# Two-layer hybrid block on one core: order of elements in a triangular inverse, and where partial sums are kept

## Chip, cores and metric

One core of a Trainium2 chip runs the whole program in one launch. The metric is the device time in microseconds, the median of several runs. Engines are named as in the profile: PE (TensorE matmul; PEld is its weight load), DVE (VectorE), ACT (ScalarE), POOL (GpSimd), SP (SyncE, which here only issues DMAs).

## What is computed

Two layers over 512 latent and 256 context tokens of width 1024. In each layer one input projection feeds three token mixers (bidirectional RWKV-7, latent attention, windowed attention), each of them gated, projected and merged:

```python
h = rms_norm(x, norm_g) * (1.0 + scale) + shift
za, ga, zb, gb, zc, gc, zg = jnp.split(h @ w_in, list(IN_CUTS), axis=-1)
# RWKV-7: S <- S diag(w) - (S kk)(kk*a)^T + v k^T ; y = S r, over time, both directions
ya, yb, yc = rwkv(za), attention(zb), window_attention(zc)
gates = sigmoid(zg)                                  # three branches x 1024 channels
m = sum(gates[n] * ((y[n] * silu(g[n])) @ w_branch_out[n]) for n in range(3))
x = x + gate * (m @ w_out)
```

The context tokens take the same way in the first layer; the second gives only the latent tokens. All is fp32.

## The kernel before

Activations lie with channels on partitions and T = 768 tokens (256 context, 512 latent) along the free axis. A matrix product splits both operands into a high part (fp32r) and a rest and adds three products (`hh,wh`, `hl,wh`, `hh,wl`), 512 and 256 columns wide. ScalarE makes the high part of the weights (L165), GpSimd the rest (L166).

The order is made by a planner: every instruction has a priority by its `band` (a lower number goes first), and the planner places it on its in-order engine by its own estimate of durations. `SERVE` is the first band; in layer 0 the scan has band 1, the heads 3, the filler 4, the end of the layer 5. A layer runs so:

1. `head` normalises; `zphase` makes the RWKV inputs and writes them to memory (`ard`, `bkd`, `vd`, and `ttd` for the triangular matrices).
2. `rwkv` scans 12 chunks of 64 tokens, 16 (head, direction) pairs at once. Groups of NS = 4 chunks share one `rwkv_inverse`, which inverts unit triangular 32x32 blocks: load `TT`, transpose (L666), mask on GpSimd (L670), 30 steps of a product and a sum on VectorE (L676, L678), two transposes (L681, L682), then small matmuls `zp` and `yp` that join two blocks to 64x64. It is a generator; `yield` marks where the caller may do something else. The inverse of group 0 stands before the scan; that of a later group is advanced at the end of each chunk of the group before, and in three steps in its last chunk. `rwkv_step` is the chain from chunk to chunk: `Rp`, `Up` (which needs `YB`, the inverse), `Sp`, with copies `UV` and the state `So` on VectorE and ScalarE. `rwkv_scores` prepares the chunk after next (`scps`, `AR`, `TR`).
3. `pace(n)` advances the filler, `tiles`, by n steps: the other projections (`zb`, `ga`, `gb`, `zc`, `gc`, then 24 of the merge gates), 8 steps to a tile; a tile of `g` kind ends in a SiLU on VectorE (`st`, L779). `FILL[l]` says how many steps stand around `zphase`, before the scan, and in each part of a chunk; `readout` runs after chunks 3, 9 and 11 and reads `ga`. What is left of the filler (`gates`) stands behind the attention heads in priority.
4. `mla` and `gqa`, the attention heads.
5. In layer 0, `later(0)` and `later(1)` run branches 0 and 1 of the merge, and `tail` branch 2 and the output product. `branch` loads a gated mixer output (`ygt`), splits it into `yh` and `yl`, multiplies by `w_bo`, and per tile of 128 channels loads the gates (`zt`), and VectorE makes the product (L1356). Branch 0 writes it to `md` in memory; branch 1 loads it back (`m`, L1364), adds (L1365) and writes the sum (L1366); `tail` loads that (L1381) and adds (L1382). Tiles `xs`, the residual stream on chip for the next layer, are allocated just before `tail`.

Pools are stacked: `bo` (with `yh`, `yl`, `ygt`, `zt`, `m0`) is opened where `hh` and `hl` were, after their last use. The next layer's conditioning (`modps`, `mod`) is interleaved with the filler, too.

Of the kernel before, what the change touches and what calls it, by code (L numbers as in the profile page):

```python
# [19 lines left out]
P = 128  # L20
# [9 lines left out]
GB, RB, CB = 2, 3, 2  # L30


FILL = ((48, 36, 2, (2, 2, 2), (3, 3, 3), 2), (72, 56, 4, (2, 2, 2), (3, 3, 3), 2))

QUEUES = (("scalar", "sync", "sync", "scalar"), ("sync", "scalar", "sync", "sync"))

# [24 lines left out]
def build(tc, A, out):  # L61
# [448 lines left out]
    def rwkv(l, D, last, DL, B, pace, zlast):  # L510

        with tc.tile_pool(name="rw", bufs=1, reuse_waits="tile") as rp:
            yo = rp.tile([P, 4, T], F32, name="yo")
            st = {"seen": set(), "S": None}
            parts, YB = {}, {}

            def scores(i):
                if i < NCH:
                    parts[i] = yield from rwkv_scores(l, last, rp, i)

            def invert(g):
                if g < NG:
                    YB[g] = rp.tile([P, 32, 64], F32, tag="YB", name="YB", bufs=2)
                    yield from rwkv_inverse(l, rp, g, YB[g])

            def rest(*gens):
                for g in gens:
                    for _ in g:
                        pass

            with band(B + 1):
                rest(scores(0), scores(1))
                ahead = invert(0)
                for _ in range(3):
                    next(ahead)
            with band(B + 4), tc.issue_after(zlast):
                pace(FILL[l][1])
            with band(B + 1), in_line():
                for _ in ahead:
                    pace(FILL[l][2])  # L540
                ahead = out = iter(())
                for i in range(NCH):
                    if i % NS == 0:
                        rest(ahead)
                        ahead = invert(i // NS + 1)
                    nxt = scores(i + 2)
                    step = rwkv_step(l, last, i, yo, st, DL, rp, parts.pop(i), YB[i // NS])
                    for n in FILL[l][3 if i % NS < NS - 1 else 4]:
                        next(step, None)
                        next(nxt, None)  # L550
                        if i % NS == NS - 1:
                            next(ahead, None)
                        next(out, None)
                        pace(n)
                    rest(step, nxt)
                    if i % NS < NS - 1:
                        next(ahead, None)
                    if i in READY and (i > 3 or not last):
                        rest(out)
                        out = readout(l, D, rp, yo, READY[i])  # L560
                for _ in out:
                    pace(FILL[l][5])

# [90 lines left out]
    def rwkv_inverse(l, rp, g, YB):  # L654
# [3 lines left out]
        for b0 in (0, 64):  # L658

            DMA.dma_start(TT[b0:b0 + 32], tt_d[l][b0:b0 + 32, :, cs])  # L660
            DMA.dma_start(TT[b0 + 32:b0 + 64, :, :, 0:32], tt_d[l][b0 + 32:b0 + 64, :, cs, 32:64])
        inv = rp.tile([P, 1536], F32, tag="inv", name="inv")
        MB, tmp = inv[:, 0:1024], inv[:, 1024:1536]
        YK = YB[:, :, 32:64]
        TT4 = TT.rearrange("p c s t -> p (c s) t")
        V.transpose(MB, TT4[:, :, 0:32].rearrange("p n j -> p j n"))  # L666

        M3 = MB.rearrange("p (j i) -> p i j", i=32)
        Y3 = YK.rearrange("p j i -> p i j")
        G.affine_select(YK, MB.rearrange("p (j i) -> p j i", i=32),  # L670
                        [[1, 32], [-1, 32]], ALU.is_gt, 0.0, base=0, channel_multiplier=0)
        V.memset(YB.rearrange("p n c -> p (n c)")[:, 32:2048:65], 1.0)
        for j in range(30, 0, -1):
            n = 31 - j
            t3 = tmp[:, 256 * (j % 2):256 * (j % 2) + j * n].rearrange("p (i c) -> p i c", c=n)
            V.tensor_tensor(t3, M3[:, 0:j, j:j + 1].to_broadcast([P, j, n]),  # L676
                            Y3[:, j:j + 1, j + 1:32].to_broadcast([P, j, n]), ALU.mult)
            V.tensor_tensor(Y3[:, 0:j, j + 1:32], Y3[:, 0:j, j + 1:32], t3, ALU.add)  # L678
            if j in (22, 12):
                yield  # L680
        V.transpose(YB[:, :, 0:32].rearrange("p n j -> p j n"), YK)  # L681
# [646 lines left out]
        turns(8, prepare, attend, later, filler)  # L1328


    def branch(l, n_, tp, segs, bank, put, lead=()):

        yh, yl = ({s0: tp.tile([P, 4, n], F32R, tag=f"{t}{s0}", name=t, bufs=1) for (s0, n) in segs} for t in ("yh", "yl"))
        with band(SERVE):
            for j in range(4):
                for (s0, n) in segs:
# [12 lines left out]
        for j in range(8):  # L1349
            yield  # L1350
            ps = finish(begun[j]) if j < len(lead) else gemm(A["w_bo"][l, n_, j], 4, yh, yl, segs, bank)
            with band(SERVE):
                for (s0, n), p_ in zip(segs, ps):
                    th = tp.tile([P, 512], F32, tag="zt", name="zt", bufs=4 if l else 5)[:, 0:n]
                    DMA.dma_start(th, th_zg[l][8 * n_ + j][:, s0:s0 + n])
                    V.scalar_tensor_tensor(th, th, 1.0, p_, ALU.add, ALU.mult)  # L1356
                    put(j, s0, n, th)

    def early(l, n_, tp, segs):

        def put(j, s0, n, t):
            if n_:
                m0 = tp.tile([P, 512], F32, tag="m0", name="m0", bufs=3)[:, 0:n]
                DMA.dma_start(m0, m_d[l][j][:, s0:s0 + n])  # L1364
                (G if l else V).tensor_tensor(t, t, m0, ALU.add)  # L1365
            DMA.dma_start(m_d[l][j][:, s0:s0 + n], t)  # L1366

        return branch(l, n_, tp, segs, "gg", put)

    def tail(l, mod, last, xs, bp):  # L1370
        segs = (LAT,) if last else (LAT, CTX)
        with tc.tile_pool(name="tailp", bufs=1, reuse_waits="tile") as tp:
# [4 lines left out]

            def put(j, s0, n, t):
                sl = slice(s0, s0 + n)
                m0 = tp.tile([P, 512], F32, tag="m0", name="m0", bufs=3)[:, 0:n]  # L1380
                DMA.dma_start(m0, m_d[l][j][:, sl])  # L1381
                V.tensor_tensor(t, t, m0, ALU.add)  # L1382
                S.copy(mh[:, j, sl], t)  # L1383
                V.tensor_tensor(ml[:, j, sl], t, mh[:, j, sl].bitcast(F32), ALU.subtract)
# [38 lines left out]
    for l in range(2):  # L1423
# [18 lines left out]
        def tiles():  # L1442
# [2 lines left out]
            zc = [(T_ZC + j, zb_d[l][4 + j], (LAT,) if last and j < 4 else BOTH, "raw") for j in range(6)]  # L1445
            ga, gb, gc = ([(t + j, g_d[l][4 * n + j], segs, "silu") for j in range(4)]
                          for n, t in enumerate((T_GA, T_GB, T_GC)))
            todo = zb[2:] + zc[4:] + zc[:4] + zb[:2] + ga + gb if last else zb + ga + gb + zc
            todo += gc + [(T_ZG + j, th_zg[l][j], segs, "tanh") for j in range(24)]
            for a in todo:  # L1450
                yield from proj(l, hh, hl, *a, side)
# [37 lines left out]

        def later(n_):  # L1490

            g = early(l, n_, bp, segs)
            with band(B + 4):
                next(g)
            for _ in range(8):
                yield
                with band(B + 4):
                    next(g, None)
# [35 lines left out]
        if not last:  # L1534
            gates()
            bp = merge_pool()
            for n_ in range(2):
                for _ in later(n_):
                    pass
# [1 line left out]
            for _ in chain(*fillers):  # L1541
                pass
        with band(B + 5):
            if not last:
                xctx = ExitStack()
                xp = xctx.enter_context(tc.tile_pool(name="xs", bufs=1, side="right"))
                xs = [xp.tile([P, T], F32, name=f"xs{k}") for k in range(KT)]
            weights["queue"] = getattr(nc, QUEUES[l][3])
            tail(l, mod, last, xs, bp)
            bctx.close()  # L1550
# [95 lines left out]
```

## Time and profile before

| | us |
|---|---|
| median of 3 runs | 2393.21 |
| lowest, highest | 2389.98, 2396.64 |
| profiled execution, its own time | 2389.18 |
| its span, first to last instruction | 2387.5 |

| engine | busy us | share |
|---|---|---|
| PE | 2104.1 | 88% |
| DVE | 1303.6 | 55% |
| ACT | 891.0 | 37% |
| POOL | 867.3 | 36% |

A share is a mean over stages. Layer 0 scans from about 415 to 680 us, runs its heads to about 1165 and merges to about 1303; layer 1 scans from about 1700 to 1920. To read a stage, take the busy time of its stretch, then PE's waits in it. PE's granted clock is given as a share of the full one.

### The profile page before, as it was taken

The numbers are of one execution on the slowest core, as the hardware profiler recorded it, in microseconds if no ns is written. First come the engines' busy times: TensorE is split into PE (matmuls) and PEld (weight loads), VectorE is DVE, ScalarE is ACT, GpSimd is POOL, SyncE is SP. The second block draws the span as 40 slices with busy tenths as digits, with TensorE's granted clock in tenths as the row PEclk, the third lists the DMA queues.
The fourth block names the chain that finished last, engine by engine and source line by source line (L and its number), as shares of the span: only waits on it lengthen the run. The fifth ranks groups of instructions, "written<-read, shape, count | busy, mean of one in ns | idle before, by whom it ended". The sixth has DMA issues, their size and how long they took to land. (4 is left out here: it accounts for less than half of the span.)

```text
span 2387.5 us, 42421 instructions
## 1 busy us (share of the span) xinstructions
PE 2104.1 (88%) x16680; PEld 1624.5 (68%) x16680; DVE 1303.6 (55%) x2300; ACT 891.0 (37%) x1654; POOL 867.3 (36%) x699
## 2 busy tenths in 40 slices
PE   6986895987998999989888998789868998999989
PEld 3865674766887766766677876567646876666657
DVE  4475326766337666247435255733678347566643
ACT  3443211233345333454213244433222356434432
POOL 1354312111123345444433324544211135556663
PEclk9998898998999999999999999999888999999999
DMA  7146575555241111531487414467444253215344
GB/s 251 58 135 183 181 199 146 150 139 134 72 161 54 67 34 54 183 98 38 142 264 227 148 56 124 137 210 189 122 110 113 82 181 105 92 49 181 107 146 145
DMA packets 330441, 314.23 MB, mean 132 GB/s; under 512 B 112768, under 2 KB 239488, under 8 KB 330240
## 3 DMA queue, kind: packets, MB, share of 16 engines
q1 hardware_dynamic: 312432, 281.87, 39.7%
q10 hardware_dynamic: 17808, 29.63, 3.9%
q8 instruction: 132, 2.16, 0.4%
q14 instruction: 69, 0.57, 0.1%
HBM read 213.64 MB, written 97.78 MB: 130 GB/s over the span
## 5 line engine op out<-in xcount | busy, mean ns | idle before, releaser
L166 POOL TENSOR_TENSOR wl<-wf,wh 128x512 fp32r<-128x512 f32 x316 | 425.9, 1350 | 1026.3 <-ACT wh L165 928.5
L154 PE MATMUL g<-hh,wh 128*128 128x512 f32 (+1 forms) x1264 | 469.9, 372 | 19.5 <-DVE st L779 10.9
L154 PE MATMUL g<-hh,wl 128*128 128x512 f32 (+1 forms) x1264 | 455.9, 361 | 2.1 <-POOL wl L166 2.0
L154 PE MATMUL g<-hl,wh 128*128 128x512 f32 (+1 forms) x1264 | 454.7, 360 | 0.0
L165 ACT CAST wh<-wf 128x512 fp32r<-128x512 f32 x316 | 195.1, 619 | 467.3 <-PE g L154 238.3
L154 PEld LDWEIGHTS g<-hh,wh 128*128 128x128 f32 x1264 | 248.7, 197 | 67.9 <-DVE st L779 12.8
L154 PEld LDWEIGHTS g<-hh,wl 128*128 128x128 f32 x1264 | 248.7, 197 | 41.4 <-issue 7.7
L154 PEld LDWEIGHTS g<-hl,wh 128*128 128x128 f32 x1264 | 249.2, 197 | 37.0 <-issue 8.7
L889 POOL TENSOR_TENSOR acc<-acc,pe 128x512 f32<-128x512 f32 (+2 forms) x128 | 145.2, 1135 | 117.0 <-ACT pe L885 97.5
L885 ACT ACTIVATE pe<-stp 128x256 f32<-128x256 f32 (+2 forms) x224 | 114.7, 522 | 187.6 <-PE stp L154 179.0
L867 DVE TENSOR_REDUCE mx<-mps 128x1 f32<-128x384 f32 (+2 forms) x256 | 124.7, 533 | 59.1 <-PE mps L154 58.2
L676 DVE TENSOR_TENSOR inv<-inv,YB 128x30 f32<-128x30 f32 (+9 forms) x180 | 90.9, 505 | 8.5 <-issue 2.3
L154 PE MATMUL yps<-pe,vh 128*64 128x256 f32 (+1 forms) x704 | 94.8, 379 | 0.1
L154 PE MATMUL g<-yh,wh 128*128 128x512 f32 (+1 forms) x224 | 81.9, 369 | 13.0 <-DVE zt L1356 6.6
L678 DVE TENSOR_TENSOR YB<-YB,inv 128x30 f32<-128x30 f32 (+9 forms) x180 | 90.4, 502 | 5.3
L154 PE MATMUL g<-yl,wh 128*128 128x512 f32 (+1 forms) x224 | 83.2, 372 | 8.5 <-POOL yl L1341 8.5
L909 DVE RECIPROCAL rec<-sps 128x256 f32<-128x256 f32 (+1 forms) x48 | 70.3, 1478 | 33.6 <-PE sps L154 33.4
L154 PE MATMUL gc<-hh,wh 128*128 128x512 f32 x192 | 77.1, 401 | 8.6 <-ACT hh L325 4.5
L889 POOL TENSOR_TENSOR acc<-pe 128x512 f32<-128x512 f32 (+1 forms) x48 | 53.7, 1118 | 83.0 <-ACT pe L885 73.9
L777 ACT ACTIVATE st<-g 128x256 f32<-128x256 f32 (+1 forms) x108 | 56.6, 524 | 71.1 <-PE g L154 70.1
L154 PE MATMUL g<-yh,wl 128*128 128x512 f32 (+1 forms) x224 | 80.5, 363 | 0.0
L642 DVE TENSOR_TENSOR AR<-scps,cst 64x256 f32<-64x256 f32 x96 | 40.1, 418 | 72.0 <-PE scps L154 70.9
(386 smaller groups left out, 4364.8 us busy)
## 6 DMA issues: line engine op xcount, KB each, us to landing
wf<-w_in SPq DMA_DIRECT2D x163, 256.0 KB, 2.9
wf<-ada_w SPq DMA_DIRECT2D x84, 256.0 KB, 4.1
wf<-w_in ACTq DMA_DIRECT2D x77, 256.0 KB, 2.9
bkd<-bk SPq DMA_DIRECT2D x16, 768.0 KB, 6.3
zt<-thzg SPq DMA_DIRECT2D x48, 256.0 KB, 3.6
wf<-w_bo SPq DMA_DIRECT2D x40, 256.0 KB, 2.8
thzg<-st SPq DMA_DIRECT2D x24, 384.0 KB, 2.4
md<-zt SPq DMA_DIRECT2D x32, 256.0 KB, 3.3
```

The costliest lines, as they stand in the source:

```text
L154: queued(TE.matmul(o, l, r, start=start, stop=stop, **kw))
L165: S.copy(wh, w32)
L166: eng.tensor_tensor(wl, w32, wh.bitcast(F32), ALU.subtract)
L642: V.tensor_tensor(AR[oth, pds, 2 * par, :], ps[oth, :, a0:a0 + 64], msk("ms", oth), ALU.mult)
L676: V.tensor_tensor(t3, M3[:, 0:j, j:j + 1].to_broadcast([P, j, n]), Y3[:, j:j + 1, j + 1:32].to_broadcast([P, j, n]), ALU.mult)
L678: V.tensor_tensor(Y3[:, 0:j, j + 1:32], Y3[:, 0:j, j + 1:32], t3, ALU.add)
L777: S.activation(t[:, sl], p, AF.Tanh, scale=0.5)
L867: V.tensor_reduce(mx, ps, AX.X, ALU.max)
L885: S.activation(e, st, AF.Exp, scale=scale)
L889: G.tensor_tensor(acc, keep.pop(0, acc), e, ALU.add)
L909: V.reciprocal(rec, sps)
```

## The change

1. The inverse's inner loop runs over i, which is contiguous, where it ran over c, which is 64 words apart in `YB`. The operand that is broadcast along the inner dimension changes from the matrix to the row factor.
2. `rwkv_inverse` yields once more, after its loads. The next group's inverse is created at the group's start, its loads at the scan's priority, its VectorE part in band B+2 at once; the call at the end of each chunk goes.
3. `FILL` of layer 0 has 48 steps before the scan where it had 36, and `zc` goes ahead of `ga` and `gb` in layer 0.
4. In layer 0 the sums of the three branches are kept in `xs`, which is now allocated before the merge: branch 0 writes its product there, branch 1 adds, `tail` reads. The traffic over `md` is gone there.
5. `yh` and `yl` have two buffers in layer 0.

```diff
-FILL = ((48, 36, 2, (2, 2, 2), (3, 3, 3), 2), (72, 56, 4, (2, 2, 2), (3, 3, 3), 2))
+FILL = ((48, 48, 2, (2, 2, 2), (3, 3, 3), 2), (72, 56, 4, (2, 2, 2), (3, 3, 3), 2))
...
                 ahead = invert(0)
-                for _ in range(3):
+                for _ in range(4):
                     next(ahead)
...
                         rest(ahead)
+
                         ahead = invert(i // NS + 1)
+                        next(ahead, None)
+                        with band(B + 2):
+                            for _ in range(3):
+                                next(ahead, None)
...
-                    if i % NS < NS - 1:
-                        next(ahead, None)
...
             DMA.dma_start(TT[b0 + 32:b0 + 64, :, :, 0:32], tt_d[l][b0 + 32:b0 + 64, :, cs, 32:64])
+        yield
...
-        M3 = MB.rearrange("p (j i) -> p i j", i=32)
-        Y3 = YK.rearrange("p j i -> p i j")
+        M3 = MB.rearrange("p (j i) -> p j i", i=32)
...
-            t3 = tmp[:, 256 * (j % 2):256 * (j % 2) + j * n].rearrange("p (i c) -> p i c", c=n)
-            V.tensor_tensor(t3, M3[:, 0:j, j:j + 1].to_broadcast([P, j, n]),
-                            Y3[:, j:j + 1, j + 1:32].to_broadcast([P, j, n]), ALU.mult)
-            V.tensor_tensor(Y3[:, 0:j, j + 1:32], Y3[:, 0:j, j + 1:32], t3, ALU.add)
+            t3 = tmp[:, 256 * (j % 2):256 * (j % 2) + j * n].rearrange("p (c i) -> p c i", c=n)
+            V.tensor_tensor(t3, M3[:, j:j + 1, 0:j].to_broadcast([P, n, j]),
+                            YK[:, j + 1:32, j:j + 1].to_broadcast([P, n, j]), ALU.mult)
+            V.tensor_tensor(YK[:, j + 1:32, 0:j], YK[:, j + 1:32, 0:j], t3, ALU.add)
...
-    def branch(l, n_, tp, segs, bank, put, lead=()):
+    def branch(l, n_, tp, segs, bank, put, lead=(), into=None):
-        yh, yl = ({s0: tp.tile([P, 4, n], F32R, tag=f"{t}{s0}", name=t, bufs=1) for (s0, n) in segs} for t in ("yh", "yl"))
+        yh, yl = ({s0: tp.tile([P, 4, n], F32R, tag=f"{t}{s0}", name=t, bufs=1 if l else 2) for (s0, n) in segs}
+                  for t in ("yh", "yl"))
...
-                    V.scalar_tensor_tensor(th, th, 1.0, p_, ALU.add, ALU.mult)
-                    put(j, s0, n, th)
+                    to = into(j)[:, s0:s0 + n] if into else th
+                    V.scalar_tensor_tensor(to, th, 1.0, p_, ALU.add, ALU.mult)
+                    put(j, s0, n, to)
...
+        def add(j, s0, n, t):
+            if n_:
+                V.tensor_tensor(sums[j][:, s0:s0 + n], sums[j][:, s0:s0 + n], t, ALU.add)
...
+        if sums:
+            return branch(l, n_, tp, segs, "gg", add, into=None if n_ else sums.__getitem__)
...
-                m0 = tp.tile([P, 512], F32, tag="m0", name="m0", bufs=3)[:, 0:n]
-                DMA.dma_start(m0, m_d[l][j][:, sl])
+                if last:
+                    m0 = tp.tile([P, 512], F32, tag="m0", name="m0", bufs=3)[:, 0:n]
+                    DMA.dma_start(m0, m_d[l][j][:, sl])
+                else:
+                    m0 = xs[j][:, sl]
...
-            todo = zb[2:] + zc[4:] + zc[:4] + zb[:2] + ga + gb if last else zb + ga + gb + zc
+            todo = (zb[2:] + zc[4:] + zc[:4] + zb[:2] if last else zb + zc) + ga + gb
...
             bp = merge_pool()
+            xctx = ExitStack()
+            xp = xctx.enter_context(tc.tile_pool(name="xs", bufs=1, side="right"))
+            xs = [xp.tile([P, T], F32, name=f"xs{k}") for k in range(KT)]
             for n_ in range(2):
                 for _ in later(n_):
                     pass
```

## Rows read from the trace of the kernel before

**Rows 1.** The page, engines: busy us, share of the span, instructions.

```profile
PE 2104.1 (88%) x16680; PEld 1624.5 (68%) x16680; DVE 1303.6 (55%) x2300; ACT 891.0 (37%) x1654; POOL 867.3 (36%) x699
```

**Rows 2.** Busy time by stretch: stretch, length, engines with instructions, granted clock, DMA.

```profile
440.00:480.00 40.00, 32.77 (x418) 26.02 (x412) 37.23 (x78) 9.34 (x20) 5.18 (x4) 0.91 0.61 162
600.00:640.00 40.00, 39.67 (x751) 34.77 (x751) 16.33 (x35) 13.41 (x25) 5.14 (x4) 1.00 0.24 74
1080.00:1120.00 40.00, 39.39 (x300) 26.87 (x300) 29.75 (x48) 17.85 (x44) 16.95 (x18) 1.00 0.15 44
1172.00:1303.00 131.00, 113.26 (x572) 93.42 (x573) 56.24 (x90) 30.77 (x60) 53.61 (x47) 0.91 0.82 258
```

**Rows 3.** PE's waits, 376 to 416 us: total us, times, longest.

```profile
PE zp L154 <- DVE inv L682: 23.3, 1, 23.3
```

**Rows 4.** PE's waits, 440 to 600 us, scan of layer 0.

```profile
PE modps L154 <- DVE mod L272: 6.3, 3, 3.1
PE modps L154 <- DVE mod L269: 4.1, 1, 4.1
PE Rp L154 <- DVE UV L714: 4.0, 1, 4.0
```

**Rows 5.** PE's waits, 1640 to 1720 us, ahead of layer 1's scan.

```profile
PE g L154 <- DVE st L779: 10.3, 3, 4.8
PE zp L154 <- issue: 4.7, 1, 4.7
```

**Rows 6.** PE's waits, 1720 to 1880 us, scan of layer 1.

```profile
PE zp L154 <- DVE inv L682: 16.5, 2, 13.9
PE scps L154 <- DVE TR L644: 9.6, 3, 4.1
```

**Rows 7.** PE's waits, 1172 to 1303 us, merge of layer 0.

```profile
PE g L154 <- DVE zt L1356: 6.6, 5, 3.0
PE g L154 <- ACT yh L1340: 6.3, 5, 4.9
PE g L154 <- POOL yl L1341: 4.7, 10, 1.6
PE gc L154 <- DVE zt L1356: 3.7, 1, 3.7
```

**Rows 8.** Timeline of DVE: start, us, engine, line, operation, out<-in, shapes.

```profile
379.58 0.15 DVE L676 TENSOR_TENSOR inv<-inv,YB 128x30 f32<-128x30 f32 x1 [0.35 <-DVE st L779]
379.77 0.19 DVE L678 TENSOR_TENSOR YB<-YB,inv 128x30 f32<-128x30 f32 x1
462.57 0.69 DVE L739 TENSOR_TENSOR So<-So,DL 128x512 f32<-128x512 f32 x1
464.27 0.60 DVE L676 TENSOR_TENSOR inv<-inv,YB 128x240 f32<-128x240 f32 x1
464.91 0.62 DVE L678 TENSOR_TENSOR YB<-YB,inv 128x240 f32<-128x240 f32 x1
1678.32 1.50 DVE L676 TENSOR_TENSOR inv<-inv,YB 128x238 f32<-128x238 f32 x1
```

**Rows 9.** DVE busy in the first inverse: L676, then L678.

```profile
379.40:412.20 32.80, 15.03 (x30) 0.76 0.65 148
379.40:412.20 32.80, 14.66 (x30) 0.76 0.65 148
```

**Rows 10.** PE in a 5 us stretch: busy, granted clock, DMA.

```profile
415.00:420.00 5.00, 4.53 (x76) 0.50 0.00 0
```

**Rows 11.** DMA from 1172 to 1303 us: total, and one group of issues.

```profile
DMA packets 24025, 33.85 MB, mean 258 GB/s; under 512 B 2667, under 2 KB 12159, under 8 KB 24017
md<-zt SPq DMA_DIRECT2D x16, 256.0 KB, 4.0
```

**Rows 12.** Timeline of PE in the filler: start, us, operation, shape.

```profile
341.36 0.40 PE L154 MATMUL g<-hh,wh 128*128 128x512 f32 x1
341.60 0.40 PE L154 MATMUL g<-hl,wh 128*128 128x512 f32 x1
```

More of the change, by code (lines that the diff above doesn't have):

```diff
@@ L1355, in branch, with early @@
                     DMA.dma_start(th, th_zg[l][8 * n_ + j][:, s0:s0 + n])
-                    V.scalar_tensor_tensor(th, th, 1.0, p_, ALU.add, ALU.mult)
-                    put(j, s0, n, th)
-    def early(l, n_, tp, segs):
+                    to = into(j)[:, s0:s0 + n] if into else th
+                    V.scalar_tensor_tensor(to, th, 1.0, p_, ALU.add, ALU.mult)
+                    put(j, s0, n, to)
+    def early(l, n_, tp, segs, sums):
+        def add(j, s0, n, t):
+            if n_:
+                V.tensor_tensor(sums[j][:, s0:s0 + n], sums[j][:, s0:s0 + n], t, ALU.add)
         def put(j, s0, n, t):
@@ L1490, in later @@
         def later(n_):
-            g = early(l, n_, bp, segs)
+            g = early(l, n_, bp, segs, () if last else xs)
             with band(B + 4):
@@ L1543, in build @@
         with band(B + 5):
[L1544 to L1547, printed above, removed]
             weights["queue"] = getattr(nc, QUEUES[l][3])
```

## Prediction

> **What bounds the kernel now.** The page comes first: PE is busy for 2104 of 2387.5 us [rows 1], so only two things can shorten the span by much: PE's idle stretches and stretches at the lower clock. The busy time by stretch then says where these lie. While the scan runs without an inverse on VectorE, PE is full (39.7 of 40 us at 600) with VectorE at 16.3 of 40; while an inverse runs beside it (440), VectorE is at 37.2 and PE at 32.8; the attention heads at 1080 are full again, and the merge of layer 0 (1172 to 1303) has PE at 113 of 131 us [rows 2]. Third, PE's waits in those stretches name who is late. Ahead of the first scan PE stands once for 23.3 us, on the last transpose of the inverse [rows 3]. In the scan of layer 0 it waits for small VectorE results (`mod`, `UV`) that are queued among the inverse's instructions, 14.4 us in three groups [rows 4]. Layer 1 repeats it: 10.3 us for the SiLU of the filler projections (`st`) and 4.7 us before the first scan [rows 5], 16.5 us for the inverse and 9.6 us for `TR` within it [rows 6]. In the merge it waits for the products with the gates (6.6 and 3.7 us) and for split rows (4.7 us) [rows 7].
>
> **Inverse, cost of one.** Its 30 steps have j(31-j) elements each, j from 30 to 1, 4960 in all, in two instructions (L676 multiplies, L678 adds). Before, the inner dimension walks c, 64 words apart in `YB`. A 240-element step took 0.60 and 0.62 us; a 30-element one with j = 30, whose elements are already neighbours, 0.15 and 0.19; a 512-element operation with neighbouring elements and an inner broadcast (L739) 0.69 [rows 8]. From 0.17 at 30 to 0.69 at 512 is 1.08 ns an element and 0.138 us fixed. New sum: 4960 x 1.08 ns = 5.4 us plus 30 x 0.138 = 4.1 us, 9.5 us for one kind, 19.0 for both. The first inverse has 15.03 + 14.66 = 29.7 us in them [rows 9]. **Each of six inverses loses about 10.7 us.** Bounds: 0 (the inner broadcast, now on the other operand, eats it) to 12. L739 has just such a broadcast and no surcharge, hence 10.7. Some steps take an extra 0.9 us, such as 1.50 us for 238 elements [rows 8]; I leave these in.
>
> Here the trace speaks against a page. The 240-element steps cost 0.2 us more than the neighbouring-element line gives (0.138 + 240 x 1.08 ns = 0.40 us) [rows 8]. The Trainium skill, "VectorE: DVE Perf Modes", section "Mode 1× (REGULAR) — the baseline", says that mode takes one result a cycle and works with any stride; by that rule the reordering would give nothing. The row decides for me, and the rule is the first rival below. For the slow steps, the skill's "SBUF — State Buffer", section "Who interferes with whom", says that a VectorE instruction with two SBUF inputs contends with GpSimd's reads; the new order would not change that, and the sum has no gain from it.
>
> **Ahead of the first scan, layer 0.** `FILL` moves 12 of the filler's steps here. A step is three 512-wide and three 256-wide matmuls; at a pitch of 0.24 us and, as an estimate, half that for the narrow ones [rows 12], 1.05 us, so 12.6 us. Inverse 10.7 shorter plus 12.6 more filler equals the 23.3 us wait [rows 3]. The two are not alike: 10.7 is off the path at once; the other 12.6 comes back only where the filler is taken away, in the attention heads, and there only while PE is the bound. It is at 39.4 of 40 us at 1080 [rows 2], but its idle gaps earlier in the heads don't shrink, so I count 70%, 9 us. **-20 us** (-10 to -23). The raw projections `zc` before the gates `ga` also take SiLU instructions off VectorE here; counted as nothing. `ga` ends after 112 filler steps, and 48+48+4+27 = 127 are out when the first readout needs it; if it were late it would cost one tile, 8.4 us, once.
>
> **Scan, layer 0.** Two inverses at 10.7 us leave a VectorE that was 93% busy [rows 2], and the inverse now stands at a lower priority (B+2) than the scan's own operations. What PE waits for here is queued behind it: 14.4 us [rows 4], of which I take three quarters, **-11 us** (0 to -14). Next late is the `AR` load. The earlier load I count as nothing: no wait in [rows 4] is on `TT`. Its four DMA issues now stand ahead of a chunk's loads on SP.
>
> **Layer 1.** Before the scan the path is the inverse; PE's 15 us [rows 5] are bounded by its 10.7: **-10 us** (0 to -15). In the scan the next inverse starts a chunk earlier and is 10.7 shorter; the 16.5 us wait should go nearly whole, and half of the 9.6 on `TR` [rows 6]: **-20 us** (-8 to -26). Each `zp` behind the inverse has `yp` and then all of the scan's `Up` waiting for it.
>
> **Merge of layer 0.** 32 writes and 32 reads of partial sums leave the SP queue and memory: 8 rows of 384 KB, four passes, 12.6 MB of the 33.9 MB that this stretch moves at 258 GB/s [rows 11]. Branch 0 multiplies straight into `xs`; the additions stay on VectorE. PE's own work is three branches of eight tiles, 12 x 0.24 + 12 x 0.12 = 4.3 us each [rows 12], 104 us in a stretch of 131. Waits of 6.6, 4.7 and 3.7 us [rows 7] are 15 us; reads and stores in front of the gates' loads and the single buffer of `yh`, `yl` cause them. **-15 us** (+10 to -25). The lower end is nearly all of 131 - 104. The upper is for the room: hh and hl free 48 KB a partition; the old pool is 24 + 8 + 10 + 6 = 48, the new one 48 + 8 + 10 = 66, so its `ygt` and `zt` now lie where the window attention's tiles were, and `xs` where its keys were. Their first loads wait, on SP, for the last head, and I price that at twice the 4.9 us that PE waits for the first `yh` now [rows 7].
>
> **Clock.** After a long wait PE's clock is granted at half (1.2 of 2.4 GHz), and the 4.5 us of work from 415 on ran so [rows 10]. Some seven waits of this size fall away or shrink; at 1 to 2 us each I take **-5 us** (0 to -15).
>
> **Sum.** -20 -11 -10 -20 -15 -5 = -81 us. Span 2387.5 to 2306.5; the profiled run is 1.7 us longer than its span, so 2308, against its own 2389.18. The median is 4 us above that run, so at its level **2312 us**.
>
> **Rivals.**
> *Strides are free, the inverse stays at 30 us.* For: the six inverses have other delays in them too. Against: 0.60 us beside the 0.40 of the line [rows 8]. Then the filler (9), the merge (15), and 8 of layer 1's scan for the earlier start remain: 32 us, **2361**. This is what the skill's rule above would give.
> *The pool's overlap takes back the merge.* For: 66 KB against 48. Against: branch 0 can't start before the filler's last tile frees hh, today either. +10 in place of -15, with the clock half gone: -54, **2339**.
> *The scan starves the inverse.* It stands behind every scan operation on VectorE; where it isn't finished by the last chunk of a group of four, PE stops at the boundary, at the 23.3 us of the one such wait that the trace has [rows 3]: four boundaries, +93; with -50 from the rest (20, 10, 15, 5) that is +43, **2436**, slower. It decides where a group leaves less VectorE free than the 19 us of an inverse. Against it: without inverse 24 of 40 us are free, and twelve chunks run from 418 to past 640 [rows 2, 3], 75 us or more for four, so some 45.
> *The gain of the scan turns into another wait* (loads of `AR`, ScalarE's copies): B and layer 1's scan give 10 instead of 31; -60, **2333**.
>
> **How the numbers follow.** Forecast 0.60; strides free 0.12; overlap 0.12; another wait 0.08; starvation 0.08. The range 2278 to 2368 reaches from 115 us down, where nearly all the favourable ends meet (-23 -14 -15 -26 -25 -15 = -118), to the strides-free case with 7 us on top; starvation and about 0.1 of the tails are left out. 0.3% is 7 us, about what a measurement here tells from no change. Slower is starvation, 0.08; the tail of the strides and overlap cases near 2393 is 0.05; faster 0.87.
>
> **What would show it.** L676 and L678 at a mean near 0.32 us, from 0.505 and 0.502. The 23.3 us wait on the inverse gone; if it has become 10 or more, the filler is short. VectorE in the scan's first 40 us below 32. Waits for `st` in layer 1 under 4 us. No `md` traffic in layer 0, the merge near 115 us, PE's first wait in it no longer than 5. If the inverse shortens and the scan does not, the scan's own chain was the bound. If PE idles more in the attention heads of layer 0, the moved filler is missed there.

## The result and the profile after

The changed kernel takes **2353.1 us** (2352.7 to 2359.8) against 2392.5 us: ratio 0.9845 [0.9829, 0.9862], 39 us less. The forecast was 2312, so the sign held and less than half of the 81 us came. The profiled execution has a span of 2351.5 us. One execution among all those of this study, of the variant with the old sums through memory, took 4867.8 us and is left out of that variant's figures.

Five views of after answer to rows of before. The page's engines [rows 1]: PE lost 7 us of busy time, VectorE 36.

```profile
PE 2096.9 (89%) x16680; PEld 1623.2 (69%) x16680; DVE 1267.4 (54%) x2300; ACT 890.7 (38%) x1654; POOL 865.6 (37%) x699
```

Busy time by stretch, columns as in [rows 2] (stretch, length, then PE, PEld, DVE, ACT and POOL with their instructions, granted clock, DMA share, GB/s), the last stretch being the merge of layer 0:

```profile
440.00:480.00 40.00, 27.22 (x343) 21.72 (x342) 34.76 (x85) 8.70 (x16) 4.57 (x4) 0.87 0.58 129
600.00:640.00 40.00, 39.89 (x700) 34.53 (x702) 16.80 (x36) 12.75 (x24) 5.75 (x5) 1.00 0.28 81
1080.00:1120.00 40.00, 39.25 (x289) 26.79 (x290) 30.31 (x47) 20.10 (x50) 17.79 (x19) 1.00 0.18 50
1155.00:1289.00 134.00, 110.86 (x625) 94.25 (x622) 67.45 (x104) 33.94 (x67) 57.89 (x50) 0.91 0.54 167
```

In the scan's first stretch PE fell from 32.8 to 27.2 us: it waits there more than before, 6.3 us for loads of `AR` and 6.3 for `mod`. PE's waits over whole stages name the reason. The lines come from five stretches (376 to 416, 440 to 600, 1640 to 1700, 1690 to 1850, 1155 to 1289 us) and answer to [rows 3 to 7] in turn:

```profile
PE zp L154 <- DVE inv L685: 2.3, 1, 2.3
...
PE scps L154 <- DMA AR<-ard: 13.5, 3, 7.2
PE modps L154 <- DVE mod L272: 6.6, 3, 6.1
...
PE zp L154 <- issue: 6.4, 1, 6.4
PE g L154 <- DVE st L782: 4.3, 2, 3.1
...
PE zp L154 <- DVE inv L685: 12.9, 2, 10.8
PE Rp L154 <- ACT UV L716: 3.9, 2, 2.5
PE scps L154 <- DVE TR L647: 2.2, 2, 2.0
...
PE g L154 <- ACT yh L1345: 17.7, 1, 17.7
PE g L154 <- DVE zt L1362: 3.5, 1, 3.5
PE g L154 <- POOL yl L1346: 1.7, 4, 0.7
```

Two waits have grown. The scan of layer 0 waits 13.5 us for loads of `AR` (3.7 before), and the merge's first matmul waits 17.7 us for a split row (4.9 before). The 23.3 us ahead of the first scan are nearly gone, yet that scan starts at 411.0 us, only 4.5 us earlier: filler has taken the place of the wait.

DMA in the merge [rows 11] fell from 33.85 to 22.37 MB, as the diff promised:

```profile
DMA packets 16078, 22.37 MB, mean 167 GB/s; under 512 B 1791, under 2 KB 8133, under 8 KB 16069
```

For the rest of the document the profiled executions are cut at five marks of PE's timeline: the first `zp` of each layer's scan, the first `krp` behind each scan, and the first `mh` matmul of layer 0. "Tail" is the time from the filler's last matmul to that `mh` and is part of the column before it. All in us; the columns without the tail add up to the span. The profiled execution of "order only" took 2360.2 us, 8 more than its median, so its stages hold some us that most of its executions do not have.

| kernel | to scan 0 | scan 0 | heads and merge 0 | (tail) | mh to scan 1 | scan 1 | rest |
|---|---|---|---|---|---|---|---|
| before | 415.5 | 293.7 | 594.8 | 136.0 | 396.2 | 255.4 | 431.9 |
| after | 411.0 | 294.0 | 583.6 | 161.7 | 388.4 | 238.9 | 435.6 |
| old element order | 420.8 | 308.1 | 587.2 | 162.2 | 395.9 | 252.5 | 435.2 |
| order only | 410.6 | 286.3 | 599.5 | 138.6 | 390.4 | 236.7 | 434.9 |
| 36 steps | 409.9 | 286.9 | 580.0 | 126.8 | 390.1 | 235.3 | 438.6 |
| 36 steps, single | 406.9 | 288.5 | 588.3 | 127.5 | 389.0 | 239.0 | 434.2 |
| 36 steps, single, queue | 401.4 | 282.1 | 581.8 | 125.3 | 390.0 | 236.8 | 437.2 |

### The profile page after: what moved, and what is told of

It reads as the page before. It is cut to its first block, busy times and chain, and to the rows that moved or that the text cites. A ratio compares the mean times of both kernels' runs of the same rounds, so it can differ in the third digit from the quotient of the medians.

```text
span 2351.5 us, 42314 instructions
## 1 busy us (share of the span) xinstructions
PE 2096.9 (89%) x16680; PEld 1623.2 (69%) x16680; DVE 1267.4 (54%) x2300; ACT 890.7 (38%) x1654; POOL 865.6 (37%) x699
## 5 line engine op out<-in xcount | busy, mean ns | idle before, releaser
L154 PE MATMUL g<-yh,wh 128*128 128x512 f32 (+1 forms) x224 | 79.3, 357 | 21.4 <-ACT yh L1345 17.7
L154 PE MATMUL gc<-hl,wh 128*128 128x512 f32 x192 | 78.1, 407 | 0.1
L154 PE MATMUL scps<-AR,BK 64*128 64x128 f32 (+1 forms) x768 | 63.0, 291 | 15.8 <-DMA AR<-ard 13.5
L679 DVE TENSOR_TENSOR inv<-inv,YB 128x30 f32<-128x30 f32 (+9 forms) x180 | 70.2, 390 | 10.7 <-issue 5.1
```

The costliest lines, as they stand in the source:

```text
L154: queued(TE.matmul(o, l, r, start=start, stop=stop, **kw))
L679: V.tensor_tensor(t3, M3[:, j:j + 1, 0:j].to_broadcast([P, n, j]), YK[:, j + 1:32, j:j + 1].to_broadcast([P, n, j]), ALU.mult)
```

## The experiments

Ratios are to the kernel before, timed on the same chip, with 95% intervals. Edits are against the changed kernel unless said otherwise.

### The order of elements, taken out and alone

Taken out:

```diff
-        M3 = MB.rearrange("p (j i) -> p j i", i=32)
+        M3 = MB.rearrange("p (j i) -> p i j", i=32)
...
+            V.tensor_tensor(t3, M3[:, 0:j, j:j + 1].to_broadcast([P, j, n]),
+                            Y3[:, j:j + 1, j + 1:32].to_broadcast([P, j, n]), ALU.mult)
+            V.tensor_tensor(Y3[:, 0:j, j + 1:32], Y3[:, 0:j, j + 1:32], t3, ALU.add)
```

> The changed kernel with the inverse's inner loop over c again, 64 words apart. Theory: the order of elements carries the 7.8 us before the scan of layer 1 and most of the 16.5 in it, and nothing in the scan of layer 0; ahead of the first scan the 2.3 us wait grows by about 10: 2378 to 2388. Rival, the earlier start and the filler carry it: 2353 to 2365.

Measured: 2398.9 us, 1.0014 [1.0000, 1.0028], above both ranges.

Alone: the kernel before with only that edit the other way round.

> The kernel before with the new order of elements in the inverse alone. L676 and L678 at 0.39 us a piece as in the changed kernel. Theory: 10 us ahead of each first scan and some 8 to 16 in the scan of layer 1, none in the scan of layer 0: 2358 to 2372. Rival, the gain needs the other parts: 2378 to 2393.

Measured: 2351.9 us, 0.9822 [0.9799, 0.9845], below both ranges. **The order alone gives all that the whole change gives; all the rest without it gives nothing.** The steps themselves came out as forecast. VectorE's timeline of after, the 240-element steps that took 0.60 and 0.62 us [rows 8]:

```profile
1721.45 0.39 DVE L679 TENSOR_TENSOR inv<-inv,YB 128x240 f32<-128x240 f32 x1
1721.87 0.41 DVE L681 TENSOR_TENSOR YB<-YB,inv 128x240 f32<-128x240 f32 x1
```

But the sum did not. The groups of these two instructions in all six inverses (count, total us, mean ns), before:

```profile
L676 DVE TENSOR_TENSOR inv<-inv,YB 128x30 f32<-128x30 f32 (+9 forms) x180 | 90.9, 505 | 8.5 <-issue 2.3 <-DVE st L779 0.6 <-DVE AR L642 0.5
L678 DVE TENSOR_TENSOR YB<-YB,inv 128x30 f32<-128x30 f32 (+9 forms) x180 | 90.4, 502 | 5.3
```

and after:

```profile
L679 DVE TENSOR_TENSOR inv<-inv,YB 128x30 f32<-128x30 f32 (+9 forms) x180 | 70.2, 390 | 10.7 <-issue 5.1 <-DVE AR L645 0.5
L681 DVE TENSOR_TENSOR YB<-YB,inv 128x30 f32<-128x30 f32 (+9 forms) x180 | 67.7, 376 | 5.2
```

Per inverse that is (90.9 + 90.4)/6 = 30.2 against (70.2 + 67.7)/6 = 23.0: **7.2 us, not 10.7**. Taking the shortest instance of each size in the timeline as its undisturbed price, an inverse costs 25.7 before and 19.1 after (forecast 19.0); 19 of the 360 steps lie over 0.5 us above that, before and after alike, with 18.6 and 18.3 us on top. The traces show what these steps have in common: all 19, before and after, begin while GpSimd makes a weight's rest (`wl`, about 1.3 us) and end within 0.5 us behind it. Of the other 341 steps only 6 before and 4 after begin beside one. GpSimd's timeline of before, beside the step of 1.50 us that begins at 1678.32 [rows 8]:

```profile
1677.86 1.52 POOL L166 TENSOR_TENSOR wl<-wf,wh 128x512 fp32r<-128x512 f32 x1 [8.25 <-ACT wh L165]
```

### The filler moved ahead of the first scan

```diff
-FILL = ((48, 48, 2, (2, 2, 2), (3, 3, 3), 2), (72, 56, 4, (2, 2, 2), (3, 3, 3), 2))
+FILL = ((48, 36, 2, (2, 2, 2), (3, 3, 3), 2), (72, 56, 4, (2, 2, 2), (3, 3, 3), 2))
```

> The changed kernel with 36 filler steps before the first scan, as before. Theory that moved filler returns nothing: PE waits some 10 to 13 us for the inverse again (23.3 less 10.7), but the filler then reaches 12 us further into the last heads and covers as much of the 17.7 us wait; 2348 to 2358. Rival, the prediction's step: the filler is worth 9 us, 2360 to 2366.

Measured: 2344.0 us, 0.9793 [0.9777, 0.9809], **9 us below the changed kernel** and below both ranges. PE's waits with 36 steps, ahead of the scan and in it:

```profile
PE zp L154 <- DVE inv L685: 16.4, 1, 16.4
...
PE scps L154 <- DMA AR<-ard: 6.0, 1, 6.0
```

The wait of 16.4 us is back, and the scan still starts at 409.9, 1.1 us earlier than with 48 steps. In both kernels it starts when the inverse ends, and filler beside the inverse slows it: it runs 374.2 to 410.9 with 48 steps (9 of its instructions above 0.75 us, SiLU products between them) and 377.7 to 409.9 with 36 (6 of them). Three of either count are transposes; the other 6 and 3 are steps beside a `wl` of GpSimd. So the moved steps fill the wait, but the scan starts no earlier. It also lasts 7 us longer, as long as the `AR` wait has grown, and ends 8 us later (705.0 against 696.8). Nor do the heads give the steps back: from the end of the scan to the last head's last matmul they take 454.8 us with 48 steps and 449.8 with 36. Busy time by stretch, first the changed kernel, whose filler ends at 1127.3 and whose last head ends at 1159.8, then the one with 36 steps, whose filler ends at 1150.3 and whose last head ends at 1146.6 (columns as in [rows 2]):

```profile
1080.00:1127.00 47.00, 46.25 (x333) 31.26 (x333) 34.92 (x56) 22.09 (x53) 18.84 (x20) 1.00 0.16 46
1127.30:1159.80 32.50, 28.37 (x208) 17.21 (x206) 20.62 (x29) 10.69 (x27) 15.40 (x16) 0.95 0.17 50
1159.80:1177.50 17.70, 0.04 (x2) 0.00 (x0) 3.50 (x6) 0.92 (x2) 0.28 (x1) 0.58 0.29 79
```

```profile
1100.00:1150.00 50.00, 49.80 (x354) 33.18 (x350) 33.30 (x49) 19.96 (x48) 21.88 (x22) 1.00 0.18 50
```

With its filler gone, PE does 28.4 of 32.5 us in the last heads, at a granted clock of 0.95; with filler left it does 49.8 of 50 at 1.00. Behind the last head it then stands for 17.7 us. That wait is hardly a price of the moved steps, since with 36 steps PE waits 15.4 us there (below). The same edit in the kernel before, 36 to 48 and nothing else:

> The kernel before with 48 filler steps in place of 36 ahead of the first scan, and nothing else. Theory (a filler step moved early is not idle time won, because the heads lack it at their end): the 23.3 us wait ahead of the scan shrinks by 10 to 12 us, the first scan starts at the same 415.5 within 3 us, the filler ends 20 to 40 us earlier, and the time is the same or up to 9 us longer: 2395 to 2404. Rival (my prediction's step, nine of 12.6 us come back): 2386.

Measured: 2396.8 us, 1.0016 [1.0000, 1.0032]. The wait for the inverse shrank to 1.1 us, the scan started 5.5 us later (421.0), and the scan lasted 311.2 in place of 293.7 us. Heads and merge took 581.9 us in place of 594.8, so here the heads did give the 12 steps back, 13 us: the first branch begins at 1164.4, among the heads, whose last matmul ends at 1191.9. The later start and the longer scan took more than that. Among PE's waits in the scan is this:

```profile
PE scps L154 <- DMA AR<-ard: 13.4, 2, 9.9
```

So the long `AR` wait comes with the 48 steps and not with the early loads: 13.4 and 13.5 us with 48 steps, in the kernel before and in the changed one, 3.7 and 6.0 with 36.

### The queue of the weight loads

From the first filler steps behind the z phase to the end of layer 0's scan, ScalarE's queue issues the weight loads in place of SP's:

```diff
-QUEUES = (("scalar", "sync", "sync", "scalar"), ("sync", "scalar", "sync", "sync"))
+QUEUES = (("scalar", "scalar", "sync", "scalar"), ("sync", "scalar", "sync", "sync"))
```

> The changed kernel with the weights of layer 0's scan issued from ACT's queue in place of SP's. Theory: the 13.5 us that PE waits for AR in the scan of layer 0 come from the SP queue, which stands behind weight loads that wait for PE; AR waits fall below 4 us and the scan of layer 0 shortens by 6 to 12 us: 2341 to 2347. Rival: the weight loads then hold up ACT's copies in the scan's chain and the time rises, 2355 to 2370.

Measured: 2353.2 us, 0.9813 [0.9792, 0.9834]: the changed kernel's median, and an interval that overlaps its own, so no gain is shown. The `AR` wait fell to one of 6.2 us and the scan to 286.0 us, but it started at 422.1 in place of 411.0. There PE waits for no inverse at all, which is over at 382.3: the 48 filler steps are the bound. The other half shows with 36 steps and single buffers (below):

> The changed kernel with 36 filler steps, single buffers for yh and yl, and the weights of the first scan's stretch issued from ScalarE's queue in place of SP's. Theory: with 36 steps PE waits only 6.0 us for AR loads in the first scan, so the queue can give 4 us at most over the kernel without it, and with 48 steps its 8 us shorter scan was paid for by a later start: 2335 within 5, no difference to the kernel with 36 steps and single buffers. Rival: the shorter scan is a gain of its own, 2328.

Measured: **2328.2 us** (2322.8 to 2334.2), 0.9728 [0.9702, 0.9753], the fastest kernel of this study, 17 us below the same kernel without the queue. The rival's time came true, but the shorter scan is only part of it: in the profiled executions the start came 5.5 us earlier, the scan was 6.4 us shorter, and heads and merge 6.5. My reason against a gain had been wrong, too. SP's issues of the four loads of `TT` that the first inverse needs (shortest, median and longest issue in ns; first and last start in us), before, after, and with ScalarE's queue:

```profile
L660 SPq DMA_DIRECT2D TT<-ttd x2: 556/594/632, 345.6 to 356.0; - x2
L661 SPq DMA_DIRECT2D TT<-ttd x2: 569/584/598, 350.7 to 370.1; - x2
```

```profile
L663 SPq DMA_DIRECT2D TT<-ttd x2: 1571/1726/1881, 343.1 to 360.7; - x2
L664 SPq DMA_DIRECT2D TT<-ttd x2: 563/576/590, 347.1 to 367.3; - x2
```

```profile
L663 SPq DMA_DIRECT2D TT<-ttd x2: 627/1066/1504, 322.3 to 326.0; - x2
L664 SPq DMA_DIRECT2D TT<-ttd x2: 596/602/608, 325.3 to 327.5; - x2
```

The change issues these loads earlier in its program, but the last of the four left SP only 2.8 us earlier. They stand among weight loads and stores on SP, which wait there for other engines. SP's longest waits of after from 340 to 370 us, and its timeline:

```profile
SPq L784 <- ACT st L778: 5.5, 2, 3.9
SPq L246 <- POOL wl L166: 4.7, 3, 2.0
SPq L162 <- PE modps L154: 4.6, 3, 3.5
```

```profile
343.07 1.57 SPq L663 DMA_DIRECT2D TT<-ttd  x1
346.26 0.34 SPq L784 DMA_DIRECT2D zbd<-st  x1
346.71 0.38 SPq L246 DMA_DIRECT2D wf<-ada_w  x1
347.14 0.59 SPq L664 DMA_DIRECT2D TT<-ttd  x1
351.20 0.34 SPq L162 DMA_DIRECT2D wf<-w_in  x1
...
360.30 0.38 SPq L246 DMA_DIRECT2D wf<-ada_w  x1
360.73 1.88 SPq L663 DMA_DIRECT2D TT<-ttd  x1
```

With the weights elsewhere the four go out within 5.2 us, the inverse is over at 380 us, and PE's waits from 340 to 425 us hold no inverse:

```profile
PE modps L154 <- DMA wf<-ada_w: 6.4, 4, 2.4
PE yp L154 <- ACT inv L697: 2.1, 2, 1.7
PE g L154 <- POOL wl L166: 0.3, 1, 0.3
```

Is it the queue alone, or the queue and the early place together? The kernel before with the new order and this queue, no early loads:

> The kernel before with the new order of elements and with the weights of the first scan's stretch on ScalarE's queue in place of SP's; no early loads, 36 filler steps, old merge. Theory (the four TT loads stood behind weight loads on SP, issued from 345.6 to 370.1 us in the kernel before, and that alone set the inverse's end): the queue alone brings the inverse forward by some 20 us, the first scan starts near 401 in place of 410.6, and the time is 10 to 15 us below the 2352 of the order alone: 2337 to 2342. Rival (the earlier place of the load in the program is needed as well): first scan at 408 or later, 2350.

Measured: 2341.3 us, 0.9778 [0.9747, 0.9808], 10.5 us below the order alone, with intervals that overlap a little. Its `TT` loads go out from 321.3 to 331.4 us; the first scan starts at 405.9, between the two forecasts, and lasts 277.0 us in place of 286.3. So the queue does it and the place in the program matters little. Its heads and merge last 597.6 us against 581.8 in the 2328 kernel, and its tail 138.5 against 125.3: I put that difference of 13 us down to the on-chip sums, though the two kernels differ in the loads and the priority too.

Then less filler, 24 steps, in the kernel of 2328 us:

> The kernel of 36 steps, single buffers and ScalarE's queue (2328.2), with 24 filler steps ahead of the first scan. Theory: its inverse is ready at 380 and PE starts the scan at 401.4 only because the filler stands in front, so 12 steps fewer start the scan 12 us earlier, near 389; but the filler there already runs 7.5 us past the last head (1140.0 to 1132.3), so the 12 steps come back one for one in front of the merge and the time is the same: 2328 within 5. Rival (steps in the heads fill idle time, an earlier scan is a gain): 2316 to 2320.

Measured: 2344.5 us, 0.9786 [0.9749, 0.9822]. Both were wrong. The scan starts 16 us earlier (385.5), lasts 11 us longer (293.0), and the filler ends 10 us later (1150.7, 20 us behind the last head); its tail is 6 us longer. Heads and merge take 603.5 us in place of 581.8, 22 us more, where 12 steps are 12.6. So the steps come back and more; what the rest is, and why the scan got longer, stays open.

### The merge and its room

The old sums through memory in the changed kernel (`yh`, `yl` single, as they were):

```diff
-                if last:
-                    m0 = tp.tile([P, 512], F32, tag="m0", name="m0", bufs=3)[:, 0:n]
-                    DMA.dma_start(m0, m_d[l][j][:, sl])
-                else:
-                    m0 = xs[j][:, sl]
+                m0 = tp.tile([P, 512], F32, tag="m0", name="m0", bufs=3)[:, 0:n]
+                DMA.dma_start(m0, m_d[l][j][:, sl])
...
-            g = early(l, n_, bp, segs, () if last else xs)
+            g = early(l, n_, bp, segs, ())
```

> The changed kernel with the merge of layer 0 as before (sums in md, one buffer of yh and yl, xs allocated before the last branch). Theory: from the first product of branch 0 to the next layer the merge gained 19.6 us and lost 8 to 13 in its start, so undoing it costs 7 to 12 us: 2360 to 2365. Rival, the merge carries most of the gain: 2370 and more. Rival, it is worth nothing as its start eats it: 2350 to 2356.

Measured: 2351.1 us, 0.9825 [0.9803, 0.9847], as the second rival has it: undoing 12.6 MB of traffic costs nothing here. The tail is 160.0 us against 161.7. What stands against the gain is the 17.7 us wait. PE's and ScalarE's timelines of after (in brackets the idle time before the instruction and what ended it):

```profile
1177.51 1.01 PE L154 MATMUL g<-yh,wh 128*128 128x256 f32 x2 [17.66 <-ACT yh L1345]
```

```profile
1176.53 0.92 ACT L1345 CAST yh<-ygt 128x512 fp32r<-128x512 f32 x2 [17.76 <-DMA ygt<-ygd]
```

SP issues that load of `ygt` at 1173.90, behind the last heads' own loads and stores. With the old merge the first branch's matmul comes at 1132.7, among the heads, at 1177.5 with the new one. Room decides it, as single buffers, whose pool takes less, show:

```diff
-tag=f"{t}{s0}", name=t, bufs=1 if l else 2)
+tag=f"{t}{s0}", name=t, bufs=1)
```

> The changed kernel with one buffer each for yh and yl, so that the pool of the merge is 24 + 8 + 10 = 42 KB a partition and fits where hh and hl were. Theory of the room: the 17.7 us that PE waits for the first yh comes from loads of ygt that lie over the window attention's tiles and wait for its last gated outputs; it falls below 6 us here and branch 0 starts inside the heads, -12 to -20 us against the changed kernel, 2333 to 2341 us. Rival, the two buffers are what shortened the merge: the wait stays or the merge itself grows by 10 us or more, 2350 to 2365.

Measured: 2349.9 us, 0.9817 [0.9795, 0.9838]; the first branch begins at 1134.5 and `mh` 8 us earlier, but the time hardly moves: heads and merge take 574.8 us, 9 less than in the changed kernel, and layer 1 takes 3.5 more. Giving the other tiles a pool of their own ahead of the split rows was the weaker form:

```diff
-            return bctx.enter_context(tc.tile_pool(name="bo", bufs=1, reuse_waits="tile"))
+            one, two = (bctx.enter_context(tc.tile_pool(name=n, bufs=1, reuse_waits="tile")) for n in ("bo", "by"))
+            class Both:
+                def tile(self, *a, tag=None, **kw):
+                    return (two if tag[0:2] in ("yh", "yl") else one).tile(*a, tag=tag, **kw)
+            return Both()
```

> The changed kernel with ygt and zt in a pool of their own, opened first, so that they lie where hh and hl were, and the doubled yh and yl behind them reach into the attention's tiles instead. Theory of the room: the first loads no longer wait for the last gated outputs; the first wait falls to 3 to 10 us, 2335 to 2345. Rival, the wait is the loads' own latency behind the last head: 17 us stay and the time is 2350 to 2356.

Measured: 2358.9 us, 0.9848 [0.9824, 0.9873]; no gain in time. The branch begins at 1166.5, but PE then stands 16.4 us for `yl`, so the wait stayed, as the rival had it. (The mean granted clock of this execution was 0.906, that of the other three 0.948 to 0.951.) Then single buffers with 36 steps, and with 42:

> The changed kernel with 36 filler steps ahead of the scan and single buffers for yh and yl of layer 0's branches. Theory (the filler moved early is missed at the end of the heads, and the first loads of the branches wait for room under the old tiles): both add up, since 36 steps leave 2344 and in that kernel the first branch still begins 15.7 us after the filler's last tile (1150.0 to 1165.7); with room it begins at about 1152, and from the last head's matmul to mh it takes some 123 us in place of 134: 2335, range 2330 to 2340. Rival (the merge is bound by PE's own work and what remains of the filler): no gain over 36 steps alone, 2344 within 3.

Measured: 2345.5 us, 0.9796 [0.9775, 0.9817]. It does not add to the 36 steps (2344.0). PE's waits in the merge with 36 steps and two buffers:

```profile
PE g L154 <- ACT yh L1345: 15.4, 1, 15.4
PE g L154 <- DVE zt L1362: 3.5, 1, 3.5
PE g L154 <- POOL yl L1346: 1.2, 2, 0.7
```

and with 36 steps and single buffers:

```profile
PE g L154 <- ACT yh L1345: 5.3, 2, 5.0
PE g L154 <- POOL yl L1346: 4.0, 7, 1.6
PE g L154 <- DVE zt L1362: 3.7, 2, 3.5
PE gc L154 <- POOL yl L1346: 1.9, 2, 1.6
```

The single buffer gives back about 10 us at the first row and pays some 5 of it in small waits; the tails are 127.5 and 126.8 us. Against 136.0 before, the on-chip sums are worth 9 us of tail once the filler reaches past the last head, whichever buffers they have.

> The changed kernel with 42 filler steps ahead of the scan and single buffers for yh and yl. Theory: the loss by moved steps sets in where the filler runs out before the last head. With 42 it would end some 10 us before it does with 36 and close to the last head's end, so the time lies between those of 36 and 48 steps with the same buffers, near the first: 2338, range 2333 to 2345. Rival (the 48 steps cost through the AR loads that queue behind weight loads in the scan, which grows step by step): halfway or worse, 2343 or more, with the scan of layer 0 at 290 us.

Measured: 2346.1 us, 0.9799 [0.9780, 0.9818]: with single buffers, 36 and 42 steps are the same, and 48 (2349.9) is 4 us above them, with intervals that overlap. So the price of the moved steps, 9 us with two buffers, is at most half of that where the first branch can fill the heads' gaps. There heads and merge take 588.3, 580.4 and 574.8 us with 36, 42 and 48 steps, so the moved steps come back, 13.5 us of them; but the scan ends 10.5 us later with 48 than with 36 (705.9 against 695.4), which takes most of it again. The theory's place for 42, near 36 steps, came true, its time of 2338 did not.

### The inverse's priority

```diff
-                        with band(B + 2):
+                        with band(B + 1):
```

> The changed kernel with the next group's inverse in the scan's own band, B+1, in place of B+2. Theory: which band it is decides little, since VectorE is full in the short first group of layer 1 in both: 2350 to 2358, and the 10.8 us wait for the inverse there stays between 8 and 13. Rival, the lower band starves the inverse there: the wait falls below 5 us and the time to 2345 or less.

Measured: 2364.5 us, 0.9864 [0.9838, 0.9889], 11 us above the changed kernel by medians, but with intervals that overlap. The profiled execution was the fastest of the four (2356.1). In it layer 1's scan lasts 243.9 in place of 238.9 us, the first scan starts 4.7 us later and is 4.3 us shorter; the 11 us have no place in it.

## Why the prediction was off

By the table, the change brought -4.5, +0.3, -11.2, -7.8, -16.5 and +3.7 us from stage to stage, 36.0 in all in the profiled executions, where the prediction had -20, -11, -15, -10, -20 and -5 for the clock. The clock is no stage of the table: PE does the same 16680 instructions in 7 us less busy time, at a mean granted clock of 0.950 in place of 0.945, and what that is worth lies inside the stages. Three steps carry the miss: the saving of an inverse (10.7 taken, 7.2 measured); the moved filler, of which 9 us were to come back and nothing did in this kernel; and two prices put too low, the `AR` wait behind the 48 steps (nothing) and the room of the merge's pool (a rival only).

**The saving of an inverse was subtracted wrongly.** I took 19.0 us, a sum of undisturbed steps, from 29.7 us, which holds the slow steps [rows 9], and wrote that I left those in. They fell out of the one side only. Undisturbed against undisturbed is 25.7 - 19.1 = 6.6, and all with all 7.2. The duration of a step (0.40 forecast, 0.41 measured) was right; the size of this term was not. That the new order would not help the slow steps was right as well: they fall on GpSimd's `wl` in both orders. Where nothing else disturbs, the wait [rows 3] shrank from 23.3 to 16.4 us with 36 steps, 6.9. The Trainium skill, "VectorE: DVE Perf Modes", section "Mode 1× (REGULAR) — the baseline", has this mode make one result a cycle and says that odd strides work in it. The first rival took that to mean that strides cost nothing, and the kernel with the old order refutes that here (0.9845 against 1.0014). The Trainium skill, "Vector Engine (DVE) Microarchitecture Reference", section "5.2 Measured stream behaviour on trn2 (trn3 not measured)", has full speed for runs of two or more adjacent 4-byte words that start on an 8-byte boundary, and a slower rate where a source or the output hops at every element, both measured on integers. The traces agree for float32: with 0.138 us fixed, 0.60 us is 1.9 ns an element, 0.41 is 1.1.

**A, ahead of the first scan: -20 forecast, -4.5 seen.** The inverse's part came as -4.9 to -5.6 (order only, 36 steps). The step that failed there is the 70% of the moved filler, 9 us that should have come back in the heads; undoing the move gained 9 in all. Of the -4.5 in the changed kernel, 2 us are an earlier start of the inverse and 2.5 its shorter run, since filler beside it slowed it (36.7 us against 39.2 before and 32.2 with 36 steps). I had read PE as full in the heads at 1080 [rows 2], which is right *because* filler stood there. The filler is what makes that stretch full; it ended 3.8 us behind the last head before (1168.4 to 1164.6) and 32.5 us ahead of it after. The heads got no shorter by that: from the scan's end to the last head they take 455.4 us before and 454.8 after. Over heads and merge, the moved steps come back where the first branch of the merge can start among the heads, 12.9 us in the kernel before (594.8 to 581.9) and 13.5 with single buffers (588.3 to 574.8), and not with two buffers (580.0 to 583.6). They also have a price in front that I had put at nothing: the scan ends 8 to 23 us later with 48 steps than with 36, in these three pairs. My own sign, that PE idles more in the heads, came true, by 4 us.

**B, scan of layer 0: -11, seen +0.3.** With 36 steps it is -6.8, near the forecast scaled by the inverse's 7.2 over 10.7. Of the three groups of [rows 4], two, 8.1 us, are gone in the changed kernel, and the `mod` of L272 stays at 6.6. The 48 steps took that back in the `AR` wait. "Next late is the `AR` load" was right, its price nothing was wrong, and the fourth rival (another wait) is what happened, in layer 0 alone: with layer 1's scan the two gave 16 us, where that rival had 10. The early load was costed at nothing and brought nothing, for a reason I had not given: its queue.

**C and D, layer 1: -10 and -20, seen -7.8 and -16.5** (-20.1 with 36 steps). The shorter inverse is the cause, but the path was another than forecast: the wait for `zp`, which should have gone nearly whole, went from 16.5 to 12.9 us only, that for `TR` from 9.6 to 2.2, and PE's busy time in this scan fell by 4.0 us (217.6 to 213.6) at a granted clock of 0.913 in place of 0.899. That the sum came near -20 is in part luck. The old order gives 395.9 and 252.5 us there, almost those of before, so the earlier start without the shorter inverse is worth 3 us, not the 8 of my first rival.

**E, merge: -15, seen -11.2 for heads and merge together**, where the forecast had -24 with the filler's 9. Each came alone: the moved steps brought 12.9 us in the kernel before, the merge 14.8 with 36 steps (580.0). Together they bring 20.0 with single buffers (574.8) and 11.2 with two. So in the changed kernel the room of the new pool takes the merge's part: the second rival, with its mechanism right (66 against 48 KB, loads of `ygt` that stand on SP behind the last heads). Its price was smaller than forecast: the old merge put back gives the same time, so gain and room cancel, where I had a loss of 10 us.

**Starvation**, the slower rival, did not occur: in the scan's own band (2364.5 us) the inverse brings no gain.

Had the filler stayed at 36, the stages -5.6, -6.8, -14.8, -6.1 and -20.1 would have stood against -11 (A without the filler), -11, -15, -10 and -20. The rest of layer 1 took 2 to 7 us more than before in all kernels of the table; what it is stays open.

## What to carry to other kernels

Filler work is a stock with a place where it runs out: before you move some of it into a wait, find where its last step stands and what else PE can do behind that point, and look at what the added steps delay in front. Two gains that were each measured alone need not add up. A load that is moved earlier in a program hardly goes earlier (2.8 us here) if its queue holds loads and stores that wait for other engines; look at the issue times on the queue, and move the others off it. When a mean holds disturbed instances, subtract disturbed from disturbed and clean from clean.

## What the runs showed of the hardware

On VectorE a 240-element f32 product or sum whose inner dimension walked 64 words took 0.60 us, with neighbouring elements 0.41, and an inner broadcast on one operand cost nothing beside that. One step in nineteen takes about 1 us longer (18.6 us over 19 steps before, 18.3 over 19 after), in either order. All of these begin beside a subtraction of GpSimd's (`wl`, 128x512, about 1.3 us) and end within 0.5 us behind it; no run took that work away.
